# A seventh buffer for raw weights, stream transfers begun a unit later, and a rewritten order of the second half-step

## The chip, the cores and the metric

The kernel runs on one NeuronCore of one Trainium2 chip. The metric is device time in microseconds of one execution, the median over runs: before the change 967.16 us (three runs: 961.47, 970.73 and 967.16).

## What is computed

One layer of a bidirectional encoder over 528 tokens (512 and 16 learned ones ahead of them) of width 1024: a half-step of a gated feed-forward net, a mixer (recurrences beside a Fourier transform), a second half-step of the same form, and a last norm. The part that the change touches most is the second half-step:

```python
def swiglu(h, w_in, w_out):
    gate, up = jnp.split(h @ w_in, 2, axis=-1)
    return (jax.nn.silu(gate) * up) @ w_out
...
h = h + jnp.concatenate([y_lru, y_four], axis=-1) @ w_out[l]
h = h + 0.5 * swiglu(rms_norm(h, norm_ffn2[l]), w_ffn2_in[l], w_ffn2_out[l])
return rms_norm(h, norm_final)[:, N_META:]
```

`w_in` is 1024 x 5632 (gate and up), `w_out` is 2816 x 1024, all in float32.

## The kernel before

**Tiles.** The stream `hall` lies in SBUF with the model's 1024 channels as 8 tiles of 128 partitions and the tokens along the free axis. The 2816 inner channels are 22 blocks f of 128. Each float32 operand is split into a rounded part and a remainder (ScalarE makes `whi` from the raw weights in L90, VectorE the remainder `wlo` in L91), and a product is three matmuls: high by high, low by high, high by low (`mm3`, L332, L334, L336).

**A pair, 84 matmuls.** From f = 2 on, gate and up of a block are one 2 x 2 block product over the two halves of the tokens and of the channels, done with seven products instead of eight (P1, P2, P6, P7, P5, P4, P3), each 12 matmuls of 256 columns. Its weights need sums. `pair_loads` loads three raw tiles from HBM on SP's queue: `a` (L105), `b` (L106), and half of `c` (L107). Then GpSimd's queue adds other weights onto `b` (L108) and `c` (L109) by accumulating transfers. `pair_blocks` splits `a` and half of `b`, adds the two tiles on VectorE (L120, L121), and then `b` and `c` are split as well. L120 is the first instruction that needs L109's result.

**A unit of the way out, 42 matmuls.** From f = 2 on, the blocks of `w_out` are handled likewise in units (`way_out`): one load of 512 KB (L296), four sums on VectorE (L146 to L149), two splits and seven products of 6 matmuls. Its results go to the stream partly by VectorE (`onto_h`, L624) and partly by way of a staging tile that ScalarE fills (`oq` after P1 in L631, `ov` after P6 and P5 in L641) and that GpSimd's queue adds to the stream: L636, issued in P2's step, and L652, issued in P4's. There are 16 units, four to a chunk of four blocks. Each unit runs beside the pairs of a later chunk.

**Buffers.** All raw weights, those of pairs and of units alike, use one pool, `wraw`, of 6 tiles of 512 KB. A load waits until the readers of its buffer's last tile are done. SP issues loads in one order, so one that waits holds up those behind it.

**Order.** `schedule2` writes out the order of the steps. From f = 7 on, each product of a pair is followed by one product of a unit, so that each step is 84 + 42 = 126 matmuls. Blocks 0 and 1 are done without the seven products ("classic"). Block 0 is done by halves of the tokens (`joined`), since the norm ahead of it is made by halves: `hook` places the second half's norm at k = 2 and k = 5 of the first half's 8. A scheduler sets the order on each engine from this, under priorities; `keep_in_program_order` fixes the order of the instructions that it is given to.

## Time and profile before

| | |
|---|---|
| runs | 961.47, 970.73, 967.16 us, median 967.16 us |
| the profiled execution | 961.03 us, span 959.3 us, mean granted clock 0.963 |
| busy: TensorE, VectorE, ScalarE, GpSimd | 892.8, 706.2, 480.0, 96.8 us |
| first half-step; mixer | about 0 to 355 us; 355 to 530 us |
| the second half-step's classic blocks, f = 2 to 6 with the first chunk's way out | 537 to 637 us |
| f = 7 to 20, from L120 of f = 7 to L120 of f = 21 | 637.2 to 901.3 us, 14 steps |
| the end (last chunk's way out, last norm) | 927 to 959 us |

Times are read on the one profiled execution, from the span's start. A view by windows gives for each stretch the busy time and the number of instructions of each engine, and the granted clock of TensorE. The waits give, for an engine's line, how long the engine was idle before it and which instruction ended that. The timeline lists single instructions. Of SP and of GpSimd's DMA instructions the time shown is that of the issue; the transfer itself lands later.

### The profile page before, as it was taken

To read this page: it belongs to the slowest core of one execution; us is meant where nothing else is said; L and a number is where in the kernel's file an instruction comes from. 1 tells how busy PE (TensorE), PEld (TensorE's weight loads), DVE (VectorE), ACT (ScalarE), POOL (GpSimd) and SP (SyncE) were. 2 spreads that over 40 slices of the span, in tenths; PEclk is the share of its full clock that TensorE was granted. 3 is DMA by queue.
4 is the path that set the end of the run, shared out by engine and by line. 5 is a ranking of instruction groups with operands and counts; after the bars stand their busy time and mean duration, and the time that the engine had idled before them with its cause. 6 is when DMAs were issued, how large, how long until landed. Compare 5 with 4: busy or idle time off the path is not lost. (4 is left out here: it accounts for less than half of the span.)

```text
span 959.3 us, 17078 instructions
## 1 busy us (share of the span) xinstructions
PE 892.8 (93%) x6806; PEld 863.8 (90%) x6806; DVE 706.2 (74%) x1226; ACT 480.0 (50%) x766; POOL 96.8 (10%) x114
## 2 busy tenths in 40 slices
PE   8998999999999999998999898798798978979797
PEld 8998999999999999998888888798798978979797
DVE  7997666777777769679875986677676776868654
ACT  7654344444444437686463464354443444545444
POOL 0111000101010000000000001111112112212100
PEclk9998999999999999999999899799988989999998
DMA  8655554556555434234232236555557646657612
GB/s 288 155 147 145 140 130 115 152 146 150 147 146 152 122 111 146 91 96 127 57 99 61 61 87 144 144 151 128 123 137 173 152 116 161 154 137 176 138 28 88
DMA packets 53744, 125.20 MB, mean 131 GB/s; under 512 B 5920, under 2 KB 12832, under 8 KB 53664
## 3 DMA queue, kind: packets, MB, share of 16 engines
q1 hardware_dynamic: 37280, 96.84, 33.0%
q0 software_dynamic: 15840, 26.75, 17.2%
q8 instruction: 53, 0.87, 0.4%
q10 hardware_dynamic: 544, 0.52, 0.2%
q14 instruction: 27, 0.22, 0.1%
HBM read 115.70 MB, written 2.10 MB: 123 GB/s over the span
## 5 line engine op out<-in xcount | busy, mean ns | idle before, releaser
L90 ACT ACTIVATE whi<-raw 128x1024 fp32r<-128x1024 f32 (+1 forms) x149 | 151.0, 1032 | 126.4 <-DVE raw L149 51.1
L91 DVE TENSOR_TENSOR wlo<-raw,whi 128x1024 fp32r<-128x1024 f32 (+1 forms) x149 | 175.2, 1193 | 26.9 <-ACT whi L90 25.0
L332 PE MATMUL pp<-th,whi 128*128 128x256 f32 (+1 forms) x468 | 135.4, 289 | 8.6 <-ACT q L574 8.6
L332 PE MATMUL pp<-xh,whi 128*128 128x256 f32 (+1 forms) x468 | 135.9, 291 | 0.6 <-ACT q L581 0.3
L334 PE MATMUL pp<-xl,whi 128*128 128x256 f32 (+1 forms) x468 | 135.0, 289 | 0.0
L336 PE MATMUL pp<-th,wlo 128*128 128x256 f32 (+1 forms) x468 | 134.6, 288 | 0.0
L334 PE MATMUL pp<-tl,whi 128*128 128x256 f32 (+1 forms) x468 | 134.3, 287 | 0.0
L336 PE MATMUL pp<-xh,wlo 128*128 128x256 f32 (+1 forms) x468 | 133.4, 287 | 0.0
L311 ACT ACTIVATE whi<-raw 128x512 fp32r<-128x512 f32 (+3 forms) x95 | 69.4, 740 | 69.6 <-PE po L334 36.4
L332 PEld LDWEIGHTS pp<-th,whi 128*128 128x128 f32 x468 | 90.2, 193 | 10.7 <-ACT q L574 9.8
L332 PEld LDWEIGHTS pp<-xh,whi 128*128 128x128 f32 x468 | 91.9, 196 | 2.0 <-ACT q L581 0.9
L334 PEld LDWEIGHTS pp<-xl,whi 128*128 128x128 f32 x468 | 91.5, 195 | 0.4
L334 PEld LDWEIGHTS pp<-tl,whi 128*128 128x128 f32 x468 | 90.3, 193 | 0.2
L336 PEld LDWEIGHTS pp<-th,wlo 128*128 128x128 f32 x468 | 90.3, 193 | 0.0
L336 PEld LDWEIGHTS pp<-xh,wlo 128*128 128x128 f32 x468 | 89.6, 192 | 0.0
L312 DVE TENSOR_TENSOR wlo<-raw,whi 128x512 fp32r<-128x512 f32 (+3 forms) x95 | 78.0, 826 | 12.2 <-ACT whi L311 11.3
L332 PE MATMUL pp<-ah,whi 128*128 128x256 f32 x224 | 66.7, 298 | 21.4 <-ACT whi L90 15.5
L332 PE MATMUL po<-ah,whi 128*128 128x264 f32 (+1 forms) x368 | 79.3, 295 | 2.3 <-ACT ah L384 2.2
L334 PE MATMUL po<-al,whi 128*128 128x264 f32 (+1 forms) x368 | 79.9, 295 | 1.1 <-DVE al L385 1.1
L336 PE MATMUL po<-ah,wlo 128*128 128x264 f32 (+1 forms) x368 | 78.6, 293 | 0.0
L336 PE MATMUL pp<-ah,wlo 128*128 128x256 f32 x224 | 66.8, 299 | 9.5 <-DVE wlo L91 9.5
L334 PE MATMUL pp<-al,whi 128*128 128x256 f32 x224 | 66.0, 295 | 5.1 <-DVE al L385 5.0
(250 smaller groups left out, 2173.2 us busy)
## 6 DMA issues: line engine op xcount, KB each, us to landing
raw<-in_w2i SPq DMA_DIRECT2D x44, 512.0 KB, 4.1
raw<-in_w1i SPq DMA_DIRECT2D x41, 512.0 KB, 3.8
raw<-in_w2i POOLq DMA_DIRECT2D x40, 256.0 KB, 5.8
raw<-in_w1i POOLq DMA_DIRECT2D x38, 256.0 KB, 5.4
raw<-in_w1o SPq DMA_DIRECT2D x32, 256.0 KB, 4.7
raw<-in_w2q SPq DMA_DIRECT2D x16, 512.0 KB, 4.4
raw<-in_wm SPq DMA_DIRECT2D x12, 512.0 KB, 3.6
raw<-in_w2i SPq DMA_DIRECT2D x20, 256.0 KB, 3.6
```

Source lines behind the costliest of these rows:

```text
L90: nc.scalar.activation(hi, raw, AF.Copy)
L91: nc.vector.tensor_tensor(lo, raw, hi.bitcast(F32), op=ALU.subtract)
L311: nc.scalar.activation(hi[:p, s], raw[:p, s], AF.Copy)
L312: nc.vector.tensor_tensor(lo[:p, s], raw[:p, s], hi[:p, s].bitcast(F32), op=ALU.subtract)
L332: nc.tensor.matmul(o, wh, xh[i], start=first, stop=False, skip_group_check=go_on)
L334: nc.tensor.matmul(o, wh, xl[i], start=False, stop=False, skip_group_check=go_on)
L336: nc.tensor.matmul(o, wl, xh[i], start=False, stop=last, skip_group_check=go_on)
```

## The change

1. **Way out to the stream.** The two accumulating transfers of a unit are no longer issued in its P2 and P4, but kept in `owed` and issued by `pay()` (L630 in the new numbering) at the start of the next unit's P1, the last at the tail. The staging tiles change with it: `q` is one half of one tile, in turns by unit, and `v` one of two tiles in turns.
2. **Buffers.** `wraw` has 7 tiles. The space comes from smaller constants, and from one `sq` tile instead of two.
3. **The first two blocks** are joined by halves of the tokens: the first half of block 0 and of block 1, then the second half of both, in four banks held together. The second half's norm stands at k = 4 of block 0 and k = 0 of block 1.
4. **The order.** `schedule2` puts P3 and P4 of f = 3 to 5, and from there of the first and the last block of each chunk, into the next block's step. The classic blocks' way out comes in one piece after P1 and P2 of f = 2 and 3. The products of units are pulled unevenly: none in the steps of f = 6, 10, 14 and 18, one or two after each product in the three blocks between. The steps of f = 6 to 9 have 84, 162, 144 and 114 matmuls, where each had 126 from f = 7 on.
5. L108, L109 and the add that follows (now L121) keep their program order.

The mixer and the first half-step keep their order but for a few rows.

```diff
-NORM_1 = [2, 5]
+NORM_1 = [(0, 4), (1, 0)]
...
-    wraw = ctx.enter_context(tc.tile_pool(name="wraw", bufs=6))
+    wraw = ctx.enter_context(tc.tile_pool(name="wraw", bufs=7))
...
-        nc.gpsimd.dma_start(b[:, :4], gate[:, 4:], accum_op=ALU.add)
-        nc.gpsimd.dma_start(c[:, :4], gate[:, :4], accum_op=ALU.add)
+        tc.keep_in_program_order(nc.gpsimd.dma_start(b[:, :4], gate[:, 4:], accum_op=ALU.add))
+        tc.keep_in_program_order(nc.gpsimd.dma_start(c[:, :4], gate[:, :4], accum_op=ALU.add))
...
-        nc.vector.tensor_tensor(b[:, 512:], b[:, 512:], c[:, :512], op=ALU.add)
+        tc.keep_in_program_order(nc.vector.tensor_tensor(b[:, 512:], b[:, 512:], c[:, :512], op=ALU.add))
...
     def schedule2():
-        f0, prev, fill = 0, None, []
+        names = ("P1", "P2", "P6", "P7", "P5", "P4", "P3")
+        f0, prev = 0, None
         for j, c in enumerate(CHUNKS2):
-            new = []
-            if j == 1:
-                new = [("out", prev, d, k) for d in range(ND) for k in range(prev[1] - prev[0])]
-            elif j > 1:
-                new = [("so", (j - 2, prev[0], dp), name) for dp in range(4) for name in ("P1", "P2", "P6", "P7", "P5", "P4", "P3")]
-            for i in range(c):
-                if f0 + i in CLASSIC2:
-                    yield "classic", f0 + i, None
-                    continue
-                for n, name in enumerate(("P1", "P2", "P6", "P7", "P5", "P4", "P3")):
-                    yield "in", f0 + i, name
-                    if i == 0 and n == 3:
-                        fill += new
-                    if j == 1:
-                        pulls = n > 2 if i == 0 else n in (0, 1, 3, 4)
-                    else:
-                        pulls = 1 + (j == len(CHUNKS2) - 1 and 0 < i < 3 and n % 2)
-                    for _ in range(min(len(fill), pulls)):
+            steps = range(f0, f0 + c)
+            if j == 0:
+                for f in steps:
+                    yield "classic", f, None
+            elif j == 1:
+                a, b = steps[:2]
+                for f in (a, b):
+                    yield "in", f, "P1"
+                    yield "in", f, "P2"
+                for d in range(ND):
+                    yield "out", prev, d
+                for f, name in ((a, "P6"), (b, "P6"), (a, "P7"), (a, "P5"), (b, "P7"), (a, "P4"), (a, "P3"), (b, "P5")):
+                    yield "in", f, name
+                fill = [("in", b, "P4"), ("in", b, "P3")]
+                pulls = [(0, 1, 1), (0, 1, 1)]
+            else:
+                fill += [("so", (j - 2, prev[0], dp), name) for dp in range(4) for name in names]
+                pulls = [(0, 1, 1), (1, 1, 1, 2, 2, 2, 2), (1, 2, 1, 1, 2, 1, 2), (2, 2, 2, 2, 1)]
+            for f, pull in zip(steps[-len(pulls):] if j else (), pulls if j else ()):
+                late = len(pull) < 7
+                for n, name in enumerate(names[:5] if late else names):
+                    yield "in", f, name
+                    for _ in range(pull[n] if n < len(pull) else 0):
                         yield fill.pop(0)
+                if late:
+                    fill[:0] = [("in", f, "P3"), ("in", f, "P4")]
             prev = (f0, f0 + c)
             f0 += c
         yield from fill
...
                     squared(f)
             quads = {}
+            owed = []
+            stage = []
+            def pay():
+                while owed:
+                    hv, x = owed.pop()
+                    tc.keep_in_program_order(nc.gpsimd.dma_start(hv, x, accum_op=add))
             def way_out(unit, name):
...
                 if name == "P1":
                     s["a22"], s["a11"], s["a12"] = block()
                     s["A"] = new()
-                    s["q"] = tmp.tile([P, T], F32, tag="rstd", bufs=1, name="oq")[:, :half]
+                    pay()
+                    if not stage:
+                        stage.extend(tmp.tile([P, T], F32, tag=x, bufs=1, name=x) for x in ("rstd", "ss", "sq"))
+                    e = dp % 2
+                    s["q"] = stage[0][:, e * half:(e + 1) * half]
+                    s["v"] = stage[1 + e][:, :n]
                     onto(s["A"], s["a11"], y(0), True)
                     nc.scalar.activation(s["q"], s["A"], AF.Copy, scale=0.5)
                 elif name == "P2":
                     ps = new()
                     onto(ps, s["a12"], y(1), True)
                     onto_h(h1[:, :half], ps, 0.5)
-                    nc.gpsimd.dma_start(h1[:, :half], s["q"], accum_op=add)
                 elif name == "P6":
                     s["s1"], s2, s["s3"], s["s4"] = block()
-                    s["v"] = tmp.tile([P, T], F32, tag="sq", bufs=2, name="ov")[:, :n]
                     onto(s["A"], s2, y(4), False)
                     nc.scalar.activation(s["v"][:, :half], s["A"], AF.Copy, scale=-0.5)
                 elif name == "P7":
...
                 elif name == "P4":
                     onto(s["D"], s["a22"], y(6), False)
                     onto_h(h2[:, :half], s["D"], -0.5)
-                    nc.gpsimd.dma_start(h2, s["v"], accum_op=add)
                 else:
                     onto(s["A"], s["s4"], y(2), False)
                     onto_h(h1[:, half:], s["A"], 0.5)
+                    owed.extend([(h2, s["v"]), (h1[:, :half], s["q"])])
                     del quads[unit]
 
             def gate_up(f, pg, pu):
...
                         midway()
                     mm3(ps, wh[:, k], wl[:, k], halves(X[k][0], n), halves(X[k][1], n), k == 0, k == ND - 1)
-            def joined(pg, pu):
-                (gh, gl), (uh, ul) = block(), block()
+            def joined(ps):
                 for j in range(2):
                     s = slice(j * half, (j + 1) * half)
-                    for k in range(ND):
-                        hook(j, k)
-                        x = [[t[:, s]] for t in X[k]]
-                        mm3([pg[0][:, s]], gh[:, k], gl[:, k], *x, k == 0, k == ND - 1)
-                        mm3([pu[0][:, s]], uh[:, k], ul[:, k], *x, k == 0, k == ND - 1)
+                    for i in range(0, len(ps), 2):
+                        if j == 0:
+                            held.append((block(), block()))
+                        for k in range(ND):
+                            hook(j, i // 2, k)
+                            x = [[t[:, s]] for t in X[k]]
+                            for p, (wh, wl) in zip(ps[i:i + 2], held[i // 2]):
+                                mm3([p[0][:, s]], wh[:, k], wl[:, k], *x, k == 0, k == ND - 1)
+            held = []
+            first = []
             out = {}
             for step in steps:
                 kind, f, d = step[:3]
...
                 elif kind == "classic":
                     if lead and f == 0:
                         ps = lead[:2]
-                    elif f == 0:
-                        ps = [banks(n, "pg"), banks(n, "pu")]
-                        joined(*ps)
+                    elif not lead:
+                        if not first:
+                            first = [banks(n, x) for _ in CLASSIC2 for x in ("pg", "pu")]
+                            joined(first)
+                        ps = first[2 * f:2 * f + 2]
                     else:
                         ps = [lead[2] if lead and f == 1 else banks(n, "pg"), banks(n, "pu")]
                         if not (lead and f == 1):
                             project(ps[0])
                         project(ps[1])
                     gate_up(f, *ps)
-                    sums_ready()
+                    if lead or f == len(CLASSIC2) - 1:
+                        sums_ready()
                 elif kind == "tail":
+                    pay()
                     tail([acts[j] for j in range(*f)], temps)
                 else:
                     if len(step) == 3 or step[3] == 0:
...
-    def hook(j, k):
-        if j == 0 and k in NORM_1:
-            norm_half(1, NORM_1.index(k))
+    def hook(j, f, k):
+        if j == 0 and (f, k) in NORM_1:
+            norm_half(1, NORM_1.index((f, k)))
```

**GpSimd's queue, transfers of f = 8 to 10 and of the first units.** Before (`raw` are the pairs' tiles, `oq` and `ov` a unit's staging tiles):

```order
L109 DMA raw_7359<-in_w2i 128x512
L652 DMA hall_80<-ov_7369 128x512
L636 DMA hall_80<-oq_7506 128x256
L108 DMA raw_7552<-in_w2i 128x512
L109 DMA raw_7553<-in_w2i 128x512
L652 DMA hall_80<-ov_7563 128x512
L636 DMA hall_80<-oq_7709 128x256
```

The same place in the change:

```order
L108 DMA raw_7369<-in_w2i 128x512
L109 DMA raw_7370<-in_w2i 128x512
L630 DMA hall_81<-rstd_7463 128x256
L630 DMA hall_81<-ss_7464 128x512
L108 DMA raw_7622<-in_w2i 128x512
L109 DMA raw_7623<-in_w2i 128x512
L630 DMA hall_81<-rstd_7463 128x256
L630 DMA hall_81<-sq_7465 128x512
```

A unit's transfer from `oq` stood ahead of the next pair's L108 and that from `ov` behind its L109. Now both stand together ahead of the next L108, but they are those of the unit before.

**VectorE, from the release of a buffer to L120 of f = 19.** Before, `raw_9538` is the tile `c` of f = 19. It was given the buffer of `raw_9342` (`a` of f = 18), whose last reader is the second row; its `b`, `raw_9537`, has the buffer of `raw_9267`, a unit's tile, read last in the first row:

```order
L91 TENSOR_TENSOR wlo_9438<-raw_9267,whi_9437 128x1024
L91 TENSOR_TENSOR wlo_9464<-raw_9342,whi_9463 128x1024
L91 TENSOR_TENSOR wlo_9487<-raw_9343,whi_9486 128x1024
L582 TENSOR_TENSOR q_9385<-q_9385,pp_9473 128x256
L624 SCALAR_TENSOR_TENSOR hall_80<-pp_9513,hall_80 128x256
L624 SCALAR_TENSOR_TENSOR hall_80<-pp_9580,hall_80 128x256
L587 TENSOR_TENSOR q_9385<-q_9385,pp_9473 128x256
L91 TENSOR_TENSOR jl_9671<-raw_9537,jh_9670 128x512
L91 TENSOR_TENSOR wlo_9545<-raw_9344,whi_9544 128x1024
L604 TENSOR_TENSOR w_9374<-q_9385 128x256
L605 TENSOR_TENSOR w_9374<-pp_9394,q_9385 128x256
L120 TENSOR_TENSOR raw_9537<-raw_9537,raw_9538 128x512
```

In the change `raw_9493` is the tile `c` of f = 19. It has the buffer of `raw_9219`, a unit's tile, which is read last 19 rows ahead of the add (L121 now). The stretch begins:

```order
L91 TENSOR_TENSOR wlo_9424<-raw_9219,whi_9423 128x1024
L581 TENSOR_TENSOR q_9422<-q_9422,pp_9455 128x256
L91 TENSOR_TENSOR wlo_9470<-raw_9195,whi_9469 128x1024
L643 SCALAR_TENSOR_TENSOR hall_81<-pp_9483,hall_81 128x256
L91 TENSOR_TENSOR wlo_9500<-raw_9373,whi_9499 128x1024
L121 TENSOR_TENSOR raw_9374<-raw_9374,raw_9375 128x512
```

and it ends:

```order
L91 TENSOR_TENSOR wlo_9597<-raw_9491,whi_9596 128x1024
L581 TENSOR_TENSOR q_9595<-q_9595,pp_9620 128x256
L598 TENSOR_TENSOR q_9422<-q_9422,pp_9547 128x256
L91 TENSOR_TENSOR jl_9601<-raw_9492,jh_9600 128x512
L615 TENSOR_TENSOR w_9404<-q_9422 128x256
L121 TENSOR_TENSOR raw_9492<-raw_9492,raw_9493 128x512
```

Between the release of `c`'s buffer and the add that needs the new `c`, VectorE had 10 instructions for f = 11, 13, 15, 17 and 19 and 13 for f = 12, 14, 16 and 18. The add of the pair before stood ahead of the release. In the change the counts are 19, 19, 31 and 23 for f = 11 to 14, the same for f = 15 to 18, and 19, 19 and 26 for f = 19 to 21; the add of the pair before now stands behind the release for f = 11, 15 and 19. The tile `b` had 11 to 14 and has 28 to 36.

## Rows read from the trace of the kernel before

**Rows 1.** The page: busy time, share of the span and instructions of each engine

```profile
PE 892.8 (93%) x6806; PEld 863.8 (90%) x6806; DVE 706.2 (74%) x1226; ACT 480.0 (50%) x766; POOL 96.8 (10%) x114
```

**Rows 2.** Windows: us, busy us by engine, granted clock, DMA share, GB/s

```profile
core 0: us, PE busy (x) PEld busy (x) DVE busy (x) ACT busy (x) POOL busy (x), PEclk, DMA share, GB/s
...
740.00:760.00 20.00, 19.28 (x163) 19.08 (x163) 18.21 (x33) 12.95 (x21) 3.04 (x4) 1.00 0.64 144
860.00:880.00 20.00, 18.68 (x158) 18.49 (x158) 19.05 (x35) 12.62 (x20) 4.42 (x5) 1.00 0.56 133
...
637.20:901.30 264.10, 227.54 (x1765) 221.85 (x1764) 189.27 (x334) 123.75 (x197) 50.17 (x57) 0.94 0.62 149
```

**Rows 3.** Waits, 637.2 to 901.3 us: engine, line, releaser: total us, times, longest

```profile
POOL hall L636 <- DMA raw<-in_w2i: 48.2, 5, 11.9
ACT whi L90 <- DVE raw L149: 45.2, 10, 7.6
DVE raw L120 <- DMA raw<-in_w2i: 36.6, 12, 6.0
POOL raw L108 <- DVE hall L624: 33.0, 5, 13.9
...
PE pp L332 <- ACT whi L90: 15.7, 7, 3.7
```

**Rows 4.** Waits of SP's queue in the same stretch

```profile
SPq L106 <- DVE wlo L91: 150.0, 12, 14.0
...
SPq L107 <- DVE wlo L91: 8.6, 12, 0.7
```

**Rows 5.** Timeline of SP's queue, f=18 and 19: start, length, instruction

```profile
831.68 0.33 SPq L107 DMA_DIRECT2D raw<-in_w2i  x1
...
849.49 0.33 SPq L107 DMA_DIRECT2D raw<-in_w2i  x1
```

**Rows 6.** Timeline of GpSimd's queue, same steps

```profile
836.53 0.87 POOL L109 DMA_DIRECT2D raw<-in_w2i  x1
...
851.92 0.88 POOL L636 DMA_DIRECT2D hall<-oq  x1 [11.83 <-DMA raw<-in_w2i]
...
853.46 1.15 POOL L109 DMA_DIRECT2D raw<-in_w2i  x1
```

**Rows 7.** Timeline of VectorE, same steps

```profile
843.35 0.69 DVE L120 TENSOR_TENSOR raw<-raw 128x512 f32<-128x512 f32 x1 [4.44 <-DMA raw<-in_w2i]
...
847.10 3.50 DVE L91 TENSOR_TENSOR wlo<-raw,whi 128x1024 fp32r<-128x1024 f32 x3 [1.12 <-ACT whi L90]
...
858.84 0.69 DVE L120 TENSOR_TENSOR raw<-raw 128x512 f32<-128x512 f32 x1 [1.30 <-DMA raw<-in_w2i]
```

**Rows 8.** Timeline of TensorE, f = 18

```profile
843.22 0.28 PE L336 MATMUL pp<-ah,wlo 128*128 128x256 f32 x1
847.12 0.39 PE L332 MATMUL pp<-ah,whi 128*128 128x256 f32 x1 [3.63 <-ACT whi L90]
```

**Rows 9.** Timeline of TensorE ahead of f = 7: first matmuls after three gaps

```profile
543.26 0.58 PE L332 MATMUL pg<-xh,whi 128*128 128x256 f32 x1 [1.02 <-ACT xh L384]
...
600.53 0.58 PE L332 MATMUL pp<-th,whi 128*128 128x256 f32 x1 [4.31 <-ACT q L574]
...
620.13 0.58 PE L332 MATMUL pp<-th,whi 128*128 128x256 f32 x1 [4.24 <-ACT q L574]
```

**Rows 10.** Windows: two stretches with or behind a gap, one at half clock

```profile
534.00:543.30 9.30, 6.25 (x47) 5.68 (x45) 8.10 (x18) 3.30 (x10) 0.00 (x0) 0.88 0.19 58
541.00:547.80 6.80, 5.77 (x19) 4.89 (x20) 6.09 (x16) 3.03 (x8) 0.27 (x1) 0.50 0.27 77
...
694.60:698.00 3.40, 3.40 (x16) 3.38 (x17) 3.14 (x5) 1.44 (x4) 0.00 (x0) 0.50 0.59 197
```

**Rows 11.** DMA issues of the page: instructions, KB each, median us to landing

```profile
raw<-in_w2i POOLq DMA_DIRECT2D x40, 256.0 KB, 5.8
...
raw<-in_w2i SPq DMA_DIRECT2D x20, 256.0 KB, 3.6
```

More of the change, by code (lines that the diff above doesn't have):

```diff
@@ L345, in times @@
             nc.vector.tensor_tensor(o, p, x, op=ALU.mult)
-    ones = const.tile([P, P], F32, name="ones")
+    warmer = xs.tile([P, P], F32, tag="th1", name="warmer")
+    nc.vector.memset(warmer, 1.0)
+    consts = const.tile([P, 2], F32, name="consts")
+    ones, epsc = consts[:, :1], consts[:, 1:]
     nc.vector.memset(ones, 1.0)
-    epsc = const.tile([P, 1], F32, name="epsc")
     nc.vector.memset(epsc, EPS)
@@ L357, in vec @@
         return V[:, VOFF[name] + i: VOFF[name] + i + 1]
-    minus = const.tile([P, 24], F32, name="minus")
+    minus = const.tile([P, 8], F32, name="minus")
     def less(name, i):
@@ L378, in encoder_layer @@
     for _ in range(WARM):
-        nc.tensor.matmul(warm[:, :P], ones, ones, start=True, stop=True)
+        nc.tensor.matmul(warm[:, :P], warmer, warmer, start=True, stop=True)
     def split_to(hi, lo, src, scale=None):
@@ L422, in sums_of, with add_square @@
         nc.vector.scalar_tensor_tensor(t4, b21, -1.0, t2, op0=ALU.mult, op1=ALU.subtract)
-    def add_square(ss, src, n, first):
+    def add_square(ss, src, n, first, tag="sq"):
         if first:
@@ L427, in add_square @@
         else:
-            sq = tmp.tile([P, T], F32, tag="sq", bufs=2, name="sq")
+            sq = tmp.tile([P, T], F32, tag=tag, bufs=1, name="sq")
             nc.scalar.activation(sq[:, :n], src, AF.Square)
@@ L437, in roots_of @@
         for j in range(k):
-            nc.tensor.matmul(sums[:m, j:j + 1], ss[:, j * m:(j + 1) * m], ones[:, :1], start=True, stop=True)
+            nc.tensor.matmul(sums[:m, j:j + 1], ss[:, j * m:(j + 1) * m], ones, start=True, stop=True)
         return root_of(tmp.tile([P, 8], F32, tag="root", name="root"), sums, m, k, width)
@@ L727, in ffn @@
                         on_done(d)
-    nc.vector.tensor_scalar(minus, V[:, :24], -1.0, None, op0=ALU.mult)
+    nc.vector.tensor_scalar(minus, V[:, :8], -1.0, None, op0=ALU.mult)
     sp4 = const.tile([P, 8], F32, name="sp4")
-    nsp8 = const.tile([P, 8], F32, name="nsp8")
-    lam = V[:, VOFF["lam"]: VOFF["lam"] + 8]
-    z = const.tile([P, 8], F32, name="z")
-    q = const.tile([P, 8], F32, name="q")
-    s2 = const.tile([P, 8], F32, name="s2")
+    nsp8 = lam = V[:, VOFF["lam"]: VOFF["lam"] + 8]
+    small = xs.tile([P, 3, 8], F32, tag="th0", name="small")
+    z, q, s2 = [small[:, i] for i in range(3)]
     nc.vector.tensor_scalar(sp4, lam, -1.0, 0.0, op0=ALU.mult, op1=ALU.max)
@@ L766, in encoder_layer @@
         if d > 0:
-            add_square(ss, h[d - 1], T, d == 1)
+            add_square(ss, h[d - 1], T, d == 1, ("sq", "rstd")[d % 2])
     add_square(ss, h[ND - 1], T, False)
@@ L1153, in add_to_sums @@
                 for j in range(m):
-                    nc.tensor.matmul(sums[j][:, :1], sq[:, j * P:(j + 1) * P], ones[:, :1], start=first, stop=last)
+                    nc.tensor.matmul(sums[j][:, :1], sq[:, j * P:(j + 1) * P], ones, start=first, stop=last)
             total = tmp.tile([P, 2, 256], F32, tag="rstd" if t0 else "ss", bufs=1, name="total")[:, :, :n]
@@ L1162, in group @@
                 if dp > 0:
-                    sq = tmp.tile([P, 2, 256], F32, tag="sq", bufs=2, name="sq")[:, :, :n]
+                    sq = tmp.tile([P, 2, 256], F32, tag="sq", bufs=1, name="sq")[:, :, :n]
                 residual(2 * dp, 2 * dp + 2, t0, t1, ps, sq)
```

## The prediction, made before the changed kernel ran

> **What bounds the kernel now.** The page comes first: TensorE is busy for 93% of the span, VectorE for 74% [rows 1]. A share over the whole span hides the stages, so the next view is that by windows. In 740 to 760 us TensorE is busy for 19.28 of 20 us with 163 matmuls, 118 ns each. Over f = 7 to 20 it has 1765 matmuls in 264.1 us, and is busy for 227.54 only [rows 2]. A step there takes 264.1 / 14 = 18.86 us, where 126 matmuls at 118.3 ns are 14.90. So 3.96 us of each step, 55 us in all, is not matmul work at full speed. Of the 55, 36.6 is idle time (264.1 less 227.54). The other 18.7 is busy time over 1765 x 0.1183 = 208.8 us: the granted clock is at its lower level in places, and 16 matmuls then fill 3.40 us, 212 ns each [rows 10]. Such stretches follow the gaps.
>
> What ends the idle time, the waits tell. VectorE's L120 waits for a transfer into a raw tile in 12 of 14 steps, 36.6 us; ScalarE's split waits 45.2 us for VectorE's sum L149, and TensorE 15.7 us for that split [rows 3]. The timeline shows one such step. L120 starts at 843.35 after 4.44 us of waiting for its transfer; the sums and splits stand behind it, and `wlo` runs until 850.6 [rows 7]. TensorE stands still from 843.22 to 847.12 [rows 8]. SP's next L107 leaves at 849.49, as a split lets go of its buffer [rows 5]; in 12 steps L106 waits 150 us for such splits, and L107 8.6 more behind it [rows 4]. L109 follows at 853.46 [rows 6], and the next L120 at 858.84, late again [rows 7]. **This is a loop**: late add, late splits, late release, late load, late add.
>
> **What the chain needs and has.** From L107's issue to L120 took 11.67 us (831.68 to 843.35) and 9.35 us (849.49 to 858.84) [rows 5, 7]; the parts are a 256 KB load at 3.6 us and an accumulation at 5.8 us [rows 11], and the issues. What it has is the work that VectorE does between the release of `c`'s buffer and the add. VectorE has 334 instructions in 14 steps [rows 2], 23.9 a step, so one per 0.62 us at a step of 14.9 us. The 10 or 13 instructions shown with the change are then 6.2 or 8.1 us, and 9.35 to 11.67 are wanted: late by 1.2 to 5.5 us, as the waits are (36.6 / 12 = 3.1 on average, 6.0 at most [rows 3]).
>
> **The change, part by part.**
>
> *Seventh buffer, order of the pairs.* The lead is now 19, 19, 31 and 23 instructions: 11.8, 11.8, 19.2 and 14.3 us at the same rate. Two of four are far above 11.67, two just above it. `b` has 28 or more, 17 us, so L106 no longer holds up L107. I take the loop as broken, with a rest in the two close cases. For the new step I take the stretch 740 to 760, where the chain hardly held anything up: 20 / 163 x 126 = 15.46 us [rows 2], and 0.14 for the rest: 15.6 us. The term is 14 x (18.86 - 15.6) = **-45.6 us**. Its ends are -55.4 (14.90 a step) and -5 (18.5 a step, a loop as long as now but for a lead of one load). I stand near the first, since the stretch is of this same kernel, with the same mix of pairs and units.
>
> *Payments a unit later.* L636 waited 48.2 us in 5 of the steps, 11.83 in the one shown, and L108 left right after it [rows 3, 6]. Now both payments wait for nothing that is not long past, and L108 is not behind ScalarE's copy. The number of transfers is unchanged. On SP no instruction is added. I cost it at nothing beyond the lead; it is part of why the lead can be used. What it moves GpSimd past: both payments stand ahead of the next L108, 2 x 0.88 us of issue [rows 6], hidden while the lead is above 11.67 us and otherwise late by as much.
>
> *First chunk's way out, f = 2 to 6.* TensorE has two gaps of 4.31 and 4.24 us [rows 9]. If a stretch as long as that after 541, 6.8 us at the lower of the two clock levels [rows 10], follows each, it makes half the progress, so 3.4 us more are lost each time: 15.4 us can go. The change puts the 16 products of the way out between P1, P2 and P6, where the wait for ScalarE's copy stood. I take **-10 us**, between 0 and -15.4; VectorE's adds for them come in one bunch, which is why I don't take all.
>
> *Joined blocks.* Ahead of 543.26 TensorE is busy for 6.25 of 9.30 us and has 6.80 us at the lower clock after 541 [rows 9, 10]: 3.05 idle and 3.4 lost, 6.4 at most. The first half of block 1, 48 matmuls or 5.7 us, now lies between the second half's sums and its first product. I take **-5 us**, ends 0 and -6.4. The constants, the fewer columns of `minus` and the program order that is pinned are costed at nothing: the first lie at the start under loads, the last repeats nearly the order that was.
>
> **The sum.** 961.03 - 45.6 - 10 - 5 = 900.4 us against the profiled execution. The median of the runs stands 0.64% above that one, so **906 us** as a median.
>
> **A rule against it.** GpSimd's issues took 0.87, 0.88 and 1.15 us [rows 6], the longest when VectorE was between two instructions: these rows show no lengthening by VectorE's work. The Trainium skill ("SBUF — State Buffer", "Who interferes with whom") says that a VectorE instruction with two inputs in SBUF contends with GpSimd's reads. By that rule a fuller VectorE would delay the accumulations. If each of the four issues of a step lost one split of VectorE (1.17 us, 3.50 / 3 [rows 7]), the two close leads would miss by about 4 us: 7 steps x 4 = 28 us, which is the second rival's time.
>
> And of the floor: 118 ns for 256 columns is what the row says [rows 2]. The Trainium skill ("TensorE: Matmul & The Clock Gate", "Back-to-back issue gap") gives 256 / 2.4 + 2.5 = 109 ns for an isolated matmul at full clock; a step would be 13.8 us as an estimate and the term larger by 15 us. The row decides.
>
> **The rivals.**
> 1. *The loop stays for the close leads* (chance 0.2). The same bytes in less time: the DMA share of 0.62 [rows 2] becomes 0.62 x 18.86 / 15.6 = 0.75, and landings may stretch. Then the 7 steps with 19 instructions stay as slow as now: 14 x 3.26 halves to -23. With -8 and -5 for the rest, 925, as a median 931. Against it: 740 to 760 ran at a DMA share of 0.64 and at full pace.
> 2. *VectorE becomes the bound* (0.14). From 860 to 880 it is busy for 19.05 of 20 us, and TensorE made 158 matmuls [rows 2], so 15.95 us a step: -40.7. The bunched adds of the first chunk give nothing back: 961.03 - 40.7 - 5 = 915, median 921. For it: 189.27 / 14 = 13.5 us of VectorE in a 15.6 us step, 87%, and the units now lie in three blocks of four. Against: the blocks with units have 140 matmuls on average, 16.6 us.
> 3. *It doesn't do what it says* (0.06). The sums of a unit, L146 to L149, stay behind late adds since the split order keeps them there, and only the two early terms come: 946, median 952.
> 4. *Slower: the staging tiles* (0.04). ScalarE's copy after P1 has to wait until the payment from the same half tile, two units before, has landed. Payments stand behind L108 and L109, which wait for raw loads: L108 waited 33.0 us in 5 steps, 6.6 each [rows 3]. If ScalarE stood still so long in each of 16 units, with TensorE behind it, 16 x 6.6 = 106 us: 900.4 + 106 = 1006, median 1012. It decides from 60.6 / 16 = 3.8 us per unit on. Against: a unit has about 15 us of work and its payment is issued one unit ahead.
>
> **Numbers.** The forecast has 0.56. All stalls gone would be 961.03 - 55.4 - 15.4 - 6.4 = 884, as a median 889: the low end. The high end takes in the first rival with some loss more: 937. The third rival, the fourth and the unluckier part of the first lie outside, about 1.5 in 10. The runs before differ by 1% among themselves, so 1% is about what can be told from no change. Faster by over 1%: the forecast, the first two rivals and a little of the third, 0.91. Within 1%: 0.05, from the third. Slower: 0.04, the fourth.
>
> **What would show it.** In the changed trace, the waits of the add (L121 now) for a raw transfer should fall from 36.6 us to under 10 over f = 7 to 20, those of L106 for a split from 150 to under 60, and TensorE should be busy for over 95% of that stretch with a granted clock above 0.97. VectorE idle while TensorE waits for a split, or a clock that still falls, would speak for the first rival; VectorE above 93% for the second; ScalarE waiting for a payment to land (a staging tile named as releaser) for the fourth. The forecast fails if the 19-instruction leads don't hold 9.35 to 11.67 us.

## The result, and the profile after

The changed kernel takes **895.0 us** as a median of four runs (892.79 to 898.1), the kernel before 966.74 us of four. The ratio is 0.926, with a 95% interval of 0.921 to 0.932. The profiled execution of the change took 898.1 us (span 896.3, mean granted clock 0.991), the highest of its four; that of before (961.03 us) lay below all of its four. Between these two executions the difference is 62.9 us.

The page of the change, busy time by engine (answers to [rows 1]):

```profile
PE 873.7 (97%) x6854; PEld 849.4 (95%) x6854; DVE 701.3 (78%) x1227; ACT 479.3 (53%) x766; POOL 96.8 (11%) x114
```

The windows of the change: first from the add (L121 now) of f = 7 to that of f = 21, as the last of [rows 2]; then from f = 8 to f = 20, twelve steps, as many as three chunks have, which the experiments use. Below them the same twelve steps of the kernel before:

```profile
617.70:835.10 217.40, 216.08 (x1782) 212.43 (x1782) 189.74 (x342) 127.02 (x201) 49.12 (x56) 1.00 0.75 177
629.00:813.70 184.70, 183.44 (x1514) 180.40 (x1514) 160.97 (x289) 105.92 (x169) 42.32 (x48) 1.00 0.76 178
```

```profile
650.06:880.92 230.86, 199.38 (x1534) 194.56 (x1535) 170.19 (x300) 109.87 (x173) 43.14 (x49) 0.93 0.61 144
```

The fourteen steps took 217.4 us where they took 264.1. TensorE is busy for 216.08 of them, at full clock. VectorE's busy time is the same (189.74 and 189.27 us), so its share rises from 72% to 87%.

The waits of the change in the same fourteen steps, for the lines of [rows 3] (the unit's last sum is L150 now):

```profile
ACT whi L90 <- DVE raw L150: 12.6, 4, 3.6
...
DVE raw L121 <- DMA raw<-in_w2i: 1.7, 1, 1.7
...
PE pp L345 <- DVE wlo L91: 0.3, 1, 0.3
```

The add waited 36.6 us in 12 steps and now 1.7 us in one; the split behind the sums 45.2 and now 12.6; TensorE for a split next to nothing. Both windows end where the add of f = 21 starts; that add waited another 5.21 us before and 2.83 us in the change. SP's L106 and L107, for [rows 4]:

```profile
SPq L107 <- DVE raw L122: 43.7, 8, 8.3
SPq L106 <- DVE wlo L91: 28.4, 7, 4.2
...
SPq L107 <- DVE wlo L91: 21.6, 3, 8.4
...
SPq L107 <- DVE q L581: 15.2, 3, 5.2
...
SPq L106 <- DVE raw L148: 8.7, 3, 2.9
...
SPq L106 <- DVE q L593: 4.2, 3, 1.4
...
SPq L106 <- ACT sq L670: 0.6, 3, 0.2
```

L106 held SP's queue for 150 us for buffers, now for 42. The wait has in part moved to L107, the load of `c`: 81 us now, where it was 21. It does little harm there, since the load still leaves early enough. One step shows how far ahead the transfers are. These are timelines of f = 18 and 19: SP's queue, GpSimd's queue, VectorE's adds (compare [rows 5 to 7]):

```profile
785.51 0.33 SPq L107 DMA_DIRECT2D raw<-in_w2i  x1
```

```profile
788.27 0.89 POOL L108 DMA_DIRECT2D raw<-in_w2i  x1 [3.33 <-DMA raw<-in_w2i]
790.99 0.88 POOL L109 DMA_DIRECT2D raw<-in_w2i  x1 [1.83 <-DVE w L535]
```

```profile
788.33 0.68 DVE L121 TENSOR_TENSOR raw<-raw 128x512 f32<-128x512 f32 x1
...
802.42 0.69 DVE L121 TENSOR_TENSOR raw<-raw 128x512 f32<-128x512 f32 x1
```

L107 of f = 19 leaves 16.9 us ahead of that pair's add. Before it was 9.35. L109 left 11.4 us ahead of the add, and GpSimd's accumulations take 5.9 us at the median of the fourteen steps: about half of that time is spare. No wait stands at either add.

The one wait inside the window stands at the add of f = 13, and there another queue decides. SP's queue, GpSimd's queue and VectorE's add:

```profile
695.25 0.33 SPq L107 DMA_DIRECT2D raw<-in_w2i  x1
```

```profile
701.51 0.86 POOL L630 DMA_DIRECT2D hall<-ss  x1 [4.14 <-ACT q L602]
702.16 1.11 POOL L108 DMA_DIRECT2D raw<-in_w2i  x1
702.80 1.38 POOL L109 DMA_DIRECT2D raw<-in_w2i  x1
```

```profile
712.55 0.69 DVE L121 TENSOR_TENSOR raw<-raw 128x512 f32<-128x512 f32 x1 [1.74 <-DMA raw<-in_w2i]
```

L107 left 17.3 us ahead of the add, as early as for f = 19. But L108 and L109 stood behind a unit's payment (L630) that was issued only at 701.51, and so L109 left 9.75 us ahead of the add.

### The profile page after: what moved, and what is told of

Its sections match the earlier page's. It is cut to its first block, busy times and chain, and to the rows that moved or that the text cites. A ratio compares the mean times of both kernels' runs of the same rounds, so it can differ in the third digit from the quotient of the medians.

```text
span 896.3 us, 17171 instructions
## 1 busy us (share of the span) xinstructions
PE 873.7 (97%) x6854; PEld 849.4 (95%) x6854; DVE 701.3 (78%) x1227; ACT 479.3 (53%) x766; POOL 96.8 (11%) x114
## 4 chain that ended last, share of the span: by engine, by line
PE 77%; DVE 10%; DMA 5%; ACT 3%; issue 3%; POOL 0%; SPq 0%; DVEq 0%; ACTq 0%; POOLq 0%
PE pp L341 15%; PE pp L345 15%; PE pp L343 15%; PE po L343 5%; PE po L345 5%; PE po L341 5%; DMA raw<-in_w2i 3%; DMA raw<-in_w1i 2%; PE pm L341 2%; PE pm L343 2%; PE pm L345 2%; DVE wlo L91 2%; PE pw L343 2%; PE pw L341 2%; PE pw L345 1%
## 5 line engine op out<-in xcount | busy, mean ns | idle before, releaser
L341 PE MATMUL pp<-xh,whi 128*128 128x256 f32 (+1 forms) x468 | 133.1, 286 | 0.5
L343 PE MATMUL pp<-xl,whi 128*128 128x256 f32 (+1 forms) x468 | 132.5, 284 | 0.0
L345 PE MATMUL pp<-th,wlo 128*128 128x256 f32 (+1 forms) x468 | 132.1, 283 | 0.0
L343 PE MATMUL pp<-tl,whi 128*128 128x256 f32 (+1 forms) x468 | 131.9, 282 | 0.0
L341 PEld LDWEIGHTS pp<-xh,whi 128*128 128x128 f32 x468 | 88.4, 189 | 2.9 <-ACT q L592 2.2
L343 PEld LDWEIGHTS pp<-xl,whi 128*128 128x128 f32 x468 | 88.5, 189 | 0.0
L345 PEld LDWEIGHTS pp<-th,wlo 128*128 128x128 f32 x468 | 87.9, 188 | 0.0
L345 PE MATMUL pp<-ah,wlo 128*128 128x256 f32 x224 | 62.4, 283 | 1.9 <-DVE wlo L91 1.9
L341 PE MATMUL pp<-ah,whi 128*128 128x256 f32 x224 | 63.2, 286 | 0.0
L343 PE MATMUL pp<-al,whi 128*128 128x256 f32 x224 | 63.0, 282 | 0.0
```

What stands on the lines that cost most here:

```text
L341: nc.tensor.matmul(o, wh, xh[i], start=first, stop=False, skip_group_check=go_on)
L343: nc.tensor.matmul(o, wh, xl[i], start=False, stop=False, skip_group_check=go_on)
L345: nc.tensor.matmul(o, wl, xh[i], start=False, stop=last, skip_group_check=go_on)
```

## Where the time went, by stages

Landmarks that both kernels have, read on the timeline of TensorE's matmuls (us from the span's start): the last product of the first half-step's way out, the last of the mixer's output, the first and the last product of a pair in the second half-step, the end. The last four columns are kernels of the next section.

| stage | before | change | change, again | six buffers | block 0 joined alone | even spread |
|---|---|---|---|---|---|---|
| to the end of the first half-step | 376.5 | 372.6 | 372.1 | 377.4 | 371.6 | 370.8 |
| mixer | 155.9 | 157.7 | 157.6 | 157.7 | 157.6 | 157.8 |
| norm and classic blocks up to the first pair | 29.8 | 27.0 | 25.4 | 26.3 | 29.0 | 25.4 |
| pairs and units | 364.3 | 305.4 | 305.0 | 320.1 | 304.7 | 298.4 |
| from there to the end | 32.8 | 33.6 | 33.7 | 33.7 | 33.5 | 33.2 |

Of the 63.0 us of span, 58.9 come from the pairs and units: 46.7 from the fourteen steps, 12.2 from what lies around them.

## The experiments

Times are compared by ratio to runs of the kernel before on the same chip. "Step" is a twelfth of the time from the add of f = 8 to the add of f = 20; the kernel before has 19.24 us there, the change 15.39. "Lead" is the number of VectorE's instructions between the release of `c`'s buffer and the add.

In the kernel before, the add waits in 11 of these twelve steps; in the change it waits 1.7 us in one.

**Six buffers.** `name="wraw", bufs=7` becomes 6.

> The changed kernel with 6 raw buffers in place of 7, all else as changed. As built, VectorE has 17, 22, 21 and 17 instructions between the release of c's buffer and the add that needs c, for f = 12, 13, 14 and 15 (19, 31, 23 and 19 with seven buffers, 13, 10, 13 and 10 in the kernel before). Theory (the lead decides): 17 instructions are 10.5 us against 9.35 to 11.67 us, so some adds wait by up to 1 us: 0 to 10 us above the changed kernel's 895, so 895 to 905; step of f = 7 to 20 15.5 to 16.2 us. Rival (the seventh buffer is what breaks the loop): the step goes back to 18 us or more, 930 or more.

Measured: 914.25 us, ratio 0.947 (0.945 to 0.949). Step 16.08 us: the loop did not come back. Over f = 7 to 20, the steps that the expectation named, it is 16.36, just above the theory's range. The total is a **miss** between the two: by ratio 15 to 20 us were lost, and 8.3 of them in the twelve steps. The landmarks above show 5 more in the first half-step, which the theory had not spoken of.

**The old order with all the rest.** `schedule2` is that of the kernel before.

> The changed kernel with the step order of the kernel before (unit products one by one, P3 and P4 in place); seven buffers, later payments, joined blocks and pinned order kept. As built, the lead of c is 9 to 11 instructions, b's 27 to 32. Theory (c's lead decides): the loop is back, step of f = 7 to 20 18 to 19 us, waits of the add for a raw transfer 25 us or more, about 935 to 945. Rival (seven buffers and payments out of the way of L108 suffice): step below 16.5 us, 895 to 912.

Measured: 935.32 us, ratio 0.969 (0.965 to 0.974). Step 17.93 us (17.06 over f = 7 to 20); the add waits in 11 of the twelve steps, 24 us in all. The loop is back, weaker than the theory said: the total falls in its range, the step and the waits just below theirs.

**The seventh buffer alone.** The old order, `joined` for block 0 alone, payments in P2 and P4, nothing pinned; the smaller constants and the staging tiles are those of the change. Against the kernel before, the edit that matters is this:

```diff
-    wraw = ctx.enter_context(tc.tile_pool(name="wraw", bufs=6))
+    wraw = ctx.enter_context(tc.tile_pool(name="wraw", bufs=7))
```

> The kernel before with the seventh buffer and the smaller constants alone: old order, block 0 joined alone, payments in P2 and P4, nothing pinned (staging tiles as in the change). As built, c's lead is 9 to 11 instructions, b's 27 to 32. Theory (c's lead decides): no gain in f = 7 to 20, step 18.3 to 19 us, 955 to 970. Rival (buffers decide): step below 16.5, 915 to 930.

Measured: 929.24 us, ratio 0.963 (0.961 to 0.965). The theory **missed**: the buffer alone gives 36 us, a total at the rival's upper end. Step 17.83 us, which neither had; over f = 7 to 20 it is 16.97 where it was 18.86. The window and the add's wait of this kernel:

```profile
630.20:844.20 214.00, 195.09 (x1529) 188.99 (x1529) 164.80 (x293) 108.78 (x171) 42.24 (x48) 0.97 0.64 157
```

```profile
DVE raw L121 <- DMA raw<-in_w2i: 24.1, 12, 5.0
```

The add still waits in nearly every step, 2.0 us each where it was 3.1. The lead of `c` is no better (9 to 11), but that of `b` is 27 to 32 for 11 to 14. L106 waited 150.0 us for buffers in the twelve steps before and waits 33 here, while L107, behind it before, now waits 142; 1.4 us of each step go. So the lead of `c` alone does not tell the step; `b`'s counts too.

**The new order alone**, with six buffers, block 0 joined alone, payments in P2 and P4, nothing pinned; constants and staging tiles as in the change.

> The kernel before with the new step order alone: six buffers, block 0 joined alone, payments in P2 and P4, nothing pinned (staging tiles as in the change). As built, c's lead is 17, 22, 21 and 17 for f = 12 to 15. Theory (c's lead decides): step 15.5 to 16.5 us, 900 to 920. Rival (it takes the buffer, or the later payments): step 17.5 us or more, 935 or more.

Measured: 912.77 us, ratio 0.946 (0.944 to 0.949), step 16.05 us. This is the time of the change with six buffers (914.25): later payments, joined blocks and pinned order together gave nothing that can be measured beside it. The window:

```profile
635.10:827.70 192.60, 186.01 (x1512) 183.53 (x1512) 161.53 (x288) 106.02 (x168) 42.24 (x48) 0.98 0.73 173
```

**One condition of the old order.** The kernel before, with a chunk's first unit begun at P1 of the pair instead of P7.

```diff
-                    if i == 0 and n == 3:
+                    if i == 0 and n == (3 if j == 1 else 0):
```

> The kernel before with one condition changed: from the third chunk on, a chunk's first unit begins beside the pair's P1 and not beside its P7. Six buffers, all else as before. As built, the lead of c is 25 and 19 instructions in turn for f = 9 to 19 (before 13 and 10), b's 31 and 26 (before 14 and 11). Theory (the lead of c and b decides): the waits of the add nearly vanish and a step of f = 8 to 20 falls from 19.2 to 15.5 to 16.2 us, 12 steps by 3.0 to 3.7 us: 36 to 44 us off, about 920 to 930. Rival (it takes the late P3 and P4, the units in three blocks of four, or the buffer): step above 18 us, above 950.

Measured: 917.02 us, ratio 0.950 (0.947 to 0.954), step 15.63 us; the total is 3 us better than the theory's range. The window and the add's wait:

```profile
648.20:835.80 187.60, 187.60 (x1561) 184.93 (x1560) 163.04 (x292) 105.48 (x172) 42.34 (x49) 1.00 0.78 182
```

```profile
DVE raw L120 <- DMA raw<-in_w2i: 1.1, 2, 0.7
```

The add of f = 20, which starts as this window ends, waits 3.09 us more, and that of f = 21 6.20. But TensorE has no idle time left in these steps, and the clock is full, with six buffers. The loop needed neither the late P3 and P4 nor the bunched units nor later payments to go: it hung on how the units lie against the pairs. What this changes, as built, is which buffers a pair's `c` and `b` take over, and so their leads (25 and 19 for 13 and 10). It also shifts a unit's sums and payments against the pair's own work, and the run does not separate the two.

**No accumulating transfers** (the kernel before without L108 and L109).

```diff
-        nc.gpsimd.dma_start(b[:, :4], gate[:, 4:], accum_op=ALU.add)
-        nc.gpsimd.dma_start(c[:, :4], gate[:, :4], accum_op=ALU.add)
+        pass
```

> The kernel before without the accumulating transfers of the pairs (L108 and L109 left out in both half-steps, so that part of the weights' sums is missing). The chain from the release of c's buffer to the add is then the 256 KB load alone, 3.6 us and its issue, against a lead of 10 or 13 instructions, 6.2 or 8.1 us. Theory (the chain of transfers against the lead): the add's waits vanish, step of f = 8 to 20 15.4 to 16.2 us, 915 to 930. Rival (the order of sums and splits on VectorE and ScalarE limits, whenever the transfers land): step above 17.5 us, above 940.

Measured: 889.59 us, ratio 0.922 (0.919 to 0.925), step 15.63 us: the old order, old buffers, old payments, and the step comes near that of the change (15.39). What limited was the chain of transfers, not the order of sums and splits in itself. Nor was it the number of bytes that went with them: the run before this one had its 15.63 us with all transfers, at a DMA share of 0.78. The total is below what was expected; the first half-step, which loses these transfers too, is 7.0 us shorter.

**One accumulation more** in the change: L109 issued twice.

```diff
         tc.keep_in_program_order(nc.gpsimd.dma_start(c[:, :4], gate[:, :4], accum_op=ALU.add))
+        tc.keep_in_program_order(nc.gpsimd.dma_start(c[:, :4], gate[:, :4], accum_op=ALU.add))
```

> The changed kernel with L109 issued twice, so that c holds a weight block one time too often and the chain is longer by one accumulation of 256 KB (5.8 us at the median, in both half-steps). It is then 15.2 to 17.5 us against leads of 19, 31, 23 and 19 instructions, 11.8, 19.2, 14.3 and 11.8 us. Theory: the adds with 19 and 23 wait again, by 3 to 6 and 1 to 3 us, of which some is absorbed: step of f = 8 to 20 from 15.4 to 16.5 to 18.5 us, 910 to 935. Rival (the chain is far from binding): step below 15.8 us, below 902.

Measured: 957.54 us, ratio 0.993 (0.989 to 0.996). Step 18.37 us, at the upper end of what was expected; the total is higher than expected. Window and waits of the twelve steps (the add is L122 here):

```profile
646.70:867.10 220.40, 192.88 (x1512) 189.14 (x1512) 162.08 (x289) 106.76 (x169) 53.15 (x60) 0.95 0.72 165
```

```profile
DVE raw L122 <- DMA raw<-in_w2i: 38.4, 11, 5.6
...
PE pp L346 <- DVE wlo L91: 18.2, 6, 4.2
```

A chain longer by one accumulation brings the whole picture of before back, in an order that had hardly any of it: the add late in 10 of 12 steps (and at the add that begins them), TensorE waiting for splits, the clock down to 0.95.

Which pairs are late was **missed**. The adds with 19 and 23 instructions of lead were expected to wait, those with 31 not. The adds with 31, f = 13 and 17, wait 5.64 and 4.58 us, as long as those with 23 (5.59 and 4.58). Of those with 19, f = 12, 16 and 20 wait 2.7 to 4.0 us, and f = 11 and 15 not at all.

**Units spread evenly** in the change.

```diff
-                pulls = [(0, 1, 1), (1, 1, 1, 2, 2, 2, 2), (1, 2, 1, 1, 2, 1, 2), (2, 2, 2, 2, 1)]
+                pulls = [(1, 2, 2, 2, 2)] * 4
```

> The changed kernel with the units' products spread evenly over the four blocks of a chunk (9 pulls a block, all blocks with P3 and P4 a step late). As built, the lead of c is 32 to 34 instructions for f = 8 to 20 (19 to 31 in the change). Theory (a lead above what the chain needs gives nothing more): within 1% of the changed kernel, 889 to 901, step of f = 8 to 20 15.1 to 15.5 us. Rival (the uneven spread itself is what makes it fast): step above 16.5 us, 910 or more.

Measured: **888.13 us**, ratio 0.921 (0.918 to 0.923): just below the theory's range, and better than the change, whose second comparison below gives 0.931 (0.927 to 0.935). Against the first, 0.926 (0.921 to 0.932), the intervals overlap. The window:

```profile
630.10:813.70 183.60, 183.56 (x1526) 181.59 (x1525) 162.37 (x291) 106.00 (x170) 42.33 (x48) 1.00 0.77 181
```

TensorE is busy for 183.56 of 183.60 us, 120 ns for each matmul, and no add waits. The step is 15.30, only 0.09 below the change's; most of what this kernel gains lies around the twelve steps.

**Payments at once** in the change: each unit's two transfers issued in P2 and P4 again.

```diff
                     onto_h(h1[:, :half], ps, 0.5)
+                    owed.append((h1[:, :half], s["q"]))
+                    pay()
...
                     onto_h(h2[:, :half], s["D"], -0.5)
+                    owed.append((h2, s["v"]))
+                    pay()
...
-                    owed.extend([(h2, s["v"]), (h1[:, :half], s["q"])])
```

> The changed kernel with the units' two transfers to the stream issued in P2 and P4 again, from the same staging tiles; the rest as changed, leads of c the same (19, 31, 23, 19). Theory (leads decide, payments only move issues of 0.9 us on GpSimd's queue): within 1% of the changed kernel, 887 to 904. Rival (later payments keep L108 from standing behind ScalarE's copy, and that is needed): 910 or more.

Measured: 902.96 us, ratio 0.937 (0.934 to 0.940), against 0.931 for the change on the same chip; the intervals overlap a little. That is within the theory's range, near its end. Step 15.72 us, and the add waits 6.3 us in four steps where the change, run beside it, has 1.8 in two. The later payments may be worth some 4 to 6 us; the runs don't settle it. Against it stands the next run: it keeps the later payments, has the same step and 6.2 us of waits, and is no slower than the change.

**Block 0 joined alone** in the change, the second half's norm at k = 2 and 5.

```diff
-NORM_1 = [(0, 4), (1, 0)]
+NORM_1 = [(0, 2), (0, 5)]
...
-                    elif not lead:
-                        if not first:
-                            first = [banks(n, x) for _ in CLASSIC2 for x in ("pg", "pu")]
-                            joined(first)
-                        ps = first[2 * f:2 * f + 2]
+                    elif f == 0:
+                        ps = [banks(n, "pg"), banks(n, "pu")]
+                        joined(ps)
...
-                    if lead or f == len(CLASSIC2) - 1:
-                        sums_ready()
+                    sums_ready()
```

> The changed kernel with block 0 alone joined by token halves, the second half's norm at k = 2 and 5, as in the kernel before; the rest as changed. Theory (the gap ahead of the second half's products comes back, 3 us idle and up to 3.4 us at the lower clock): 3 to 7 us above the changed kernel, 898 to 903. Rival (the sums' wait stays in both, nothing to win): within 2 us of it.

Measured: 897.94 us, ratio 0.932 (0.929 to 0.935), and the change beside it 897.26: no difference that can be measured, so the theory **missed** and the rival is met. In the profile the stage has 29.0 us against 25.4 to 27.0, and the step is 15.72 us. TensorE's waits there, with block 0 alone and then in the change:

```profile
536.67 0.58 PE L449 MATMUL sums<-consts,ss 128*128 128x1 f32 x4 [1.48 <-DVE ss L441]
537.80 0.71 PE L467 MATMUL rs<-ident,root 128*128 128x128 f32 x4 [0.55 <-DVE root L461]
...
539.83 0.39 PE L341 MATMUL pg<-xh,whi 128*128 128x256 f32 x1 [1.32 <-ACT xh L395]
```

```profile
537.73 0.58 PE L449 MATMUL sums<-consts,ss 128*128 128x1 f32 x4 [1.49 <-DVE ss L441]
```

The two later waits go, the first and longest, for the sum of squares, stays. Behind it the granted clock fell to its lower level in the first of the change's two profiles (0.50 from 539.6 to 543.0 us; the stage took 27.0) and not in the other (25.4).

**The even spread with six buffers.**

> The kernel of the even spread (units' products over all four blocks) with 6 raw buffers instead of 7. As built, the lead of c is 20 and 24 instructions in turn, 12.4 and 14.9 us, b's 32 to 34. Theory (lead above 11.67 us is enough, the buffer gives nothing of its own): within 1% of the even spread with seven buffers, 884 to 897. Rival (the seventh buffer is worth some 20 us as between the changed kernel and the one with six): 900 or more.

Measured: 900.81 us, ratio 0.935 (0.932 to 0.938): the total is a **miss** for the theory and meets the rival's. The step is 15.29 us, as with seven: there the buffer gives nothing, as the theory has it. But the whole kernel is slower by 1.4 points of ratio. Of 13.6 us in the profiles, 6.4 are lost by the end of the first half-step (377.2 against 370.8); the rest lies around f = 2 to 7, where one gap of 3.3 us at 627 has the lower clock behind it. In this order the buffer's worth is in other stages than the one for which the theory counted leads.

**The change once more.**

> The changed kernel itself once more, on the same chip as the three others, to compare them with. Every theory: 890 to 900.

Measured: 897.26 us, ratio 0.931 (0.927 to 0.935).

The first half-step, 20 to 200 us, with the matmuls that TensorE got done: before, in the change, and in the even spread with six buffers:

```profile
20.00:200.00 180.00, 175.16 (x1407) 173.40 (x1406) 136.26 (x221) 85.89 (x126) 19.35 (x22) 0.98 0.57 145
```

```profile
20.00:200.00 180.00, 177.14 (x1443) 175.47 (x1442) 139.81 (x225) 87.21 (x128) 20.66 (x24) 1.00 0.59 150
```

```profile
20.00:200.00 180.00, 174.84 (x1402) 173.16 (x1401) 135.53 (x220) 84.95 (x125) 19.38 (x22) 0.98 0.57 145
```

The 36 matmuls more are the 4 us that seven buffers give there; with six the stage is as before. Nearly all of it lies between 85 and 100 us. Before, and in the change:

```profile
85.00:100.00 15.00, 11.61 (x72) 11.20 (x71) 7.18 (x13) 3.77 (x5) 1.75 (x2) 0.77 0.57 132
```

```profile
85.00:100.00 15.00, 13.79 (x111) 13.37 (x111) 9.66 (x16) 5.37 (x8) 1.74 (x2) 1.00 0.60 145
```

A late add stands there as well. Before, on VectorE and on TensorE:

```profile
87.45 0.69 DVE L120 TENSOR_TENSOR raw<-raw 128x512 f32<-128x512 f32 x1 [4.50 <-DMA raw<-in_w1i]
```

```profile
89.87 0.51 PE L332 MATMUL po<-ah,whi 128*128 128x264 f32 x2 [2.25 <-ACT ah L384]
```

In the change this add waits 2.35 us, and TensorE has neither this gap nor the lower clock behind it.

## Why the prediction was right, and where it was not

**The steps of f = 7 to 20: right in mechanism and size.** Forecast 15.6 us a step and -45.6; measured 217.4 / 14 = 15.53 and -46.7. Of the 46.7, 35.2 were idle time of TensorE and 11.5 busy time. The chain from a released buffer to the add, measured against the time that VectorE gives it, is shown from both sides: take the accumulations away and the old order runs at 15.63, add one and the new order falls back to 18.37. All of the signs named beforehand came: the add's wait from 36.6 to 1.7 us, L106's from 150 to 42, TensorE busy for 99% at full clock.

**Most of what was credited to buffer and order together belongs to the order.** The step "seventh buffer, order of the pairs" took both as one. Before: 19.24. New order alone: 16.05. Seventh buffer alone: 17.83. Both: 15.39. So the order takes 3.2 us off a step by itself, the buffer 1.4 by itself and 0.7 beside the order. And a single condition of the old order gives 15.63 with six. The prediction read the leads off the built order, so its number held for a cause that it had not separated.

**Lead as a count: it did not tell which pairs are tight.** The rate of 0.62 us an instruction was a mean. For f = 19 the change's 19 instructions lasted 16.9 us, 0.89 each; for f = 20 another 19 lasted 9.63 us (L107 at 804.11, the add at 813.74), 0.51 each. The second is at the low end of the 9.35 to 11.67 us that the prediction took for the chain, and that add did not wait. The one add that waited in the window, f = 13, has 31 instructions and 17.3 us of lead. With six buffers the adds with 17 wait at f = 12, 16 and 20 (8.1 us in all), those with 17 at f = 15 and 19 not. The rows of before held a sign of it: f = 18, with 13 instructions, waits 4.44 us, and f = 19, with 10, only 1.30 [rows 7]. The count orders the kernels well, but not fully: 9 to 11 with `b` early ran at 17.83, 10 and 13 with `b` late at 19.24.

**Early blocks: -10 forecast, -12.2 measured**, with the last block's share in it. Ahead of the add of f = 7 alone it is -14.6 (75.0 to 60.4 us from the first product of a pair), near the end of -15.4 that the prediction gave; behind the add of f = 21, 2.4 us were lost. The gaps of 4.31 and 4.24 us became one of 1.4.

**Joined blocks: mis-sized.** Forecast -5. The stage got shorter by 2.8 to 4.4 us in profiles, and without the joined block 1 no loss could be measured in the runs. The prediction had counted on most of the three waits (3.05 us) and of the lower clock behind them; the 1.49 us for the sum of squares stands ahead of the products that were moved in.

**Costed at nothing, and wrong: the first half-step.** It is shorter by 3.9 us. The seventh buffer serves that stage too, where SP's loads use the same pool; the prediction looked for its effect in the second half-step only. The kernels with seven buffers end this stage at 370.5 to 372.7 us, those with six at 375.6 to 377.4 (leaving aside the two with an accumulation less or more). The mixer gave 1.8 back. It takes 157.6 to 157.8 us in every kernel with the smaller constants and the new staging tiles, the buffer alone and the order alone among them, and 155.9 to 156.0 in those without; which of the two costs that was not tried.

**The payments** were costed at nothing beyond the lead, since they would "wait for nothing that is not long past". The trace says otherwise. Ahead of L630, GpSimd's queue stood idle for 86 us in the fourteen steps (166 ahead of L636 and L652 before), and for f = 13 the payment held L108 and L109 until 702.16. Whether issuing them late gains anything is open: 4 to 6 us by one pair of runs, nothing by another.

**The scale.** The terms made -60.6 us against the profiled execution, where -62.9 came. That they fit so well is in part luck: 2.2 us too much for the joined blocks and 2.1 left out in the first half-step and the mixer nearly cancel. The 906 was higher than 895 mostly because 0.64% were added for a profiled run below its median; the change's profiled run was above its own.

**The rivals.** Landings did not stretch with the fuller DMA engines (share 0.75 for 0.62): in the fourteen steps an accumulation landed after 5.9 us at the median, 6.0 before. VectorE came to 87% as worked out, and TensorE was idle for 1.3 us of 217.4. The sums of a unit did not stay behind late adds: the split's wait for them fell to 12.6 us. No wait in the second half-step is put down to the landing of a payment. The Trainium skill's rule in "SBUF — State Buffer", "Who interferes with whom", by which VectorE's instructions with two inputs in SBUF contend with GpSimd's reads, does not show here: over the fourteen steps the issues of L108 and L109 took 0.98 and 1.00 us at the mean before, and 0.94 and 1.02 us in the change with VectorE busier. That the issue of a transfer is a read of the kind that the rule means was the prediction's assumption. The 28 us that it set down for this case would give 928 us, near the first rival's time and not, as it says, the second's.

## What to carry to other kernels

When a load waits for a buffer that the late work itself releases, look for the loop: take the chain from release to first use from the trace, and count what the waiting engine does in between; both ends can be tried by leaving a transfer out and by doubling one. The count is a first guess: read the time of each pair as well, and look on the queues of the chain for other transfers that stand in front. Which tile inherits which buffer follows from the order of allocation, so shifting one stream of work against another by a few steps can do more than a further buffer. And a buffer added to a pool acts in every stage that uses the pool: check those as well.

## What was not expected of the hardware

The DMA engines moved 181 GB/s at a share of 0.77 in the even spread, where it was 149 at 0.62 in the kernel before, and an accumulation of 256 KB was no slower for it (5.1 us at the median of the even spread's twelve steps, 6.0 in the fourteen of before).

TensorE's 118 ns a matmul, the pace of [rows 2], was not reached as a mean: with next to no idle time, 1526 matmuls took 183.56 us, 120 ns each. The floor of 14.90 us a step that the prediction worked out from it was not reached either; the best step is 15.29.
